# A two-layer encoder in one kernel: the PSUM banks of the first Strassen sums, two late steps, and the first loads

## The chip, the cores and the metric

The kernel runs as one program on one core of a Trainium2 chip. The metric is device time in microseconds (us) of one execution, taken as the median of the runs. The core's engines have their own instruction queues and run side by side: TensorE (PE, with PEld for its weight loads) multiplies, ScalarE (ACT) and VectorE (DVE) do the elementwise work, GpSimd (POOL) and SyncE (SP) mostly issue transfers (DMAs). PE writes its results into PSUM, which the kernel uses as eight banks of 128 x 512 floats; ACT and DVE read them there. Within an engine the instructions run in the order in which they stand; between engines they wait on semaphores.

## The reference

The input is `x` (256 tokens, 2048 features), with 256 memory tokens `mem`. Two layers follow each other. In each, one input projection feeds 12 mixer heads and 4 heads that attend to the memory; the outputs are concatenated, projected by `w_o` and added to `x`; then a squared-ReLU MLP of width 8192 is added.

```
m = rms_norm(mem, mem_norm); h = x
for i in range(2):
    n = rms_norm(h, attn_norm[i]);  z = n @ w_in[i]
    mix = neighbourhood_attention(q, k, v, rpb)      # layer 0
        | gqa_block_attention(rope(norm(q)), rope(norm(k)), v)   # layer 1
    km, vm = split(m @ w_mem_kv[i]);  cross = memory_attention(qm, km, vm)
    h = h + concat([mix, cross]) @ w_o[i]
    n = rms_norm(h, mlp_norm[i])
    h = h + square(relu(n @ w_up[i])) @ w_down[i]
return rms_norm(h, final_norm)
```

Everything is float32 in and out.

## The kernel before

**Arithmetic.** Every operand of a matmul is split into a rounded high part and the rest (`split`, L301 to L304: ACT copies into the high part, DVE subtracts for the low part), and a product is the sum of high x high, high x low and low x high. So each weight, once loaded, costs an ACT and a DVE instruction before PE can use it.

**Chunks and grains.** The weights come in chunks of 1 MB (128 x 2048 floats). The list `plan` holds the chunks in the order of use; `halves_of` turns each into two grains, `run_all` runs through the grains. A grain has up to three preparing stages (load, pre, prep) which are emitted some grains ahead of its products. `later(n, ...)` puts an emission off by n grains ("ticks"). Emission gives priority only: a scheduler then lays the instructions of each engine in the order in which, by its own timeline, their inputs are ready, so that a step emitted later need not end up later in its queue. `pin` and `past` (with `issue_after`) hold an order by hand.

**The head.** `begin` (L227) treats the first three chunks (columns of `w_km0`, the memory keys of layer 0) specially. The memory (`memT`, 2 MB) is loaded in eight slices into the room of `h`, and the three chunks in four quarters each into the three buffers `raw` of the ring pool, all issued on SP (L115 to L125). ACT and DVE make `memT` hi and lo (L329, L330) and the chunks' `hi` and `lo`; PE runs the three chunks a quarter at a time (L221, L224). The fourth chunk and those after it are loaded by `prep` in `halves_of` (L157) into the ring's three buffers, as these come free. `x_load` later uses the two buffers with the tag `l4` of the pool `work` for x transposed.

**Attention.** `attention` emits three steps for each head: `attend` (scores, exponentials), `attend2` (transposes of the probabilities and their split into `pT`), `attend3` (the value product `av`, L392 to L394, split into `cat`). In layer 1 this is called by `b_q_done` for three blocks of four heads, with `w_o` right behind.

**Residual and guard.** `o_done` adds the output projection to `h` (`add`, L650) and sums the squares of the new columns (`squares`, L592). For the last 512 columns these two and `inv` (L638 to L641) come off the path: the MLP starts from a scale taken from the first three quarters, and `later(4 | 6 | 8, past, ...)` emits them within the first grains of the MLP.

**The MLP.** `w_up` runs in eight parts of eight 128-column chunks (`u_products`, L702 to L704). Part 0 takes its PSUM tiles from the pool `ps_acc` (four banks in turn) beside `ps_att` (the other four). Each result is read by a Relu on ACT (L756), squared (L757), and turned into the left factors of a Strassen product. From the first grain of part 1 on, the two pools are closed and `ps_sums` is opened over the same eight banks: one tile `up` for `ps_u`, and seven sums `p1` to `p7`. `down_grains` runs `w_down` with seven products a step: `FIRST` (p3, p1, p2; L816 to L818 out of `bh`, `bl`), then `SECOND` (p5, p7, p6, p4 out of `th`, `tl`). A sum's tile is taken from the pool when its first product is run, so the banks are given in the order up, p3, p1, p2, p5, p7, p6, p4. A tile placed in a bank waits for the last reader of the tile that had the bank before; the last tile of part 0 (its eighth chunk) lies in the second bank, the one that p3 gets.

Of the kernel before, what the change touches and what calls it, by code (L numbers as in the profile page):

```python
# [17 lines left out]
P = 128  # L18
# [55 lines left out]
def encoder_kernel(ctx: ExitStack, tc: tile.TileContext, t: dict, out: bass.AP):  # L74
# [44 lines left out]
    for j in range(8):  # L119
        s = slice(j * 512, (j + 1) * 512)  # L120
        nc.sync.dma_start(mem0[:, s], t["memT"][:, s])
        if j % 2 == 0:
            s = slice(j * 256, (j + 2) * 256)
            for c in range(FIRST_CHUNKS):
                nc.sync.dma_start(raws[c][:, s], t["w_km0"][c][:, s])  # L125
    ident = const.tile([P, P], F32, name="ident")
    ones = const.tile([P, P], F32, name="ones")
    nc.gpsimd.memset(ones, 1.0)
# [15 lines left out]
    def halves_of(w):  # L144

        tiles = {}

        def load():
            tiles["raw"] = loaded(w.src, "U")

        def prep_early(hf):
            tiles[hf] = half_of_side(tiles["raw"], hf, MOVING_AT)

        def prep(hf):
            if hf == 0:
                tiles["raw"] = at.ring.tile([P, CH], F32, tag="raw", bufs=3, name="raw")
                nc.sync.dma_start(tiles["raw"], w.src)  # L157
            tiles[hf] = new_half()
            split(*tiles[hf], tiles["raw"][:, hf * HALF : (hf + 1) * HALF])

        def run(hf):
            if hf == 0:
                w.start(w)
            hi, lo = tiles.pop(hf)
            if w.kind == "S":
                s_products(w, hf * (KT // 2), KT // 2, hi, lo)
            else:
                for i in range(NT):
                    m_products(w, w.first + 2 * hf, 2, i, hi, lo, w.begins and hf == 0, w.last and hf == 1)

        def after():
            if w.last:
                w.done(w)
            if w.early == "last":
                to_work()

        if w.early:
            return [Grain(lambda: run(0), None, load, None, lambda: prep_early(0), SOON),
                    Grain(lambda: run(1), after, None, None, lambda: prep_early(1), SOON)]
        return [Grain(lambda: run(0), None, None, None, lambda: prep(0)),  # L180
                Grain(lambda: run(1), after, None, None, lambda: prep(1))]
# [212 lines left out]
            nc.tensor.matmul(av[:, :SEQ], v(1, k), pT[:, 0, k, :], start=False, stop=k == NT - 1)  # L394
        split(cat[:, head, :SEQ], cat[:, head, SEQ:], av[:, :SEQ])

    def attention(jobs, at, gap=1, lag=1):

        def step(n, job, prev):
            qT, kT, bias, v, head, cat = job  # L400
            if n == 0:
                res = attend(qT, kT, bias)
            elif n == 1:
                res = attend2(prev)
            else:
                return attend3(prev, v, head, cat)
            results[n, head] = res

        results = {}
        for t in range(len(jobs) + 2):  # L410
            for n in range(3):
                if 0 <= t - n < len(jobs):
                    j = t - n
                    later(at + gap * j + lag * n,
                          lambda n=n, job=jobs[j]: step(n, job, results.get((n - 1, job[4]))))


# [191 lines left out]
    def o_done(layer, nb):  # L609
        which = 2 * layer  # L610

        def guard():

            box["near"] = mean_square(which, GUARD, "near")
            box["scale"] = keep.tile([P, NT], F32, tag="scale", name="scale")
            nc.gpsimd.tensor_tensor(box["scale"], box["near"], mhalf[:, :NT], op=ALU.pow)
            box["hT"] = wide(f"hT{layer}")

        def begun():

            y = at.side.tile([P, NT, 512], F32, tag="T", bufs=2, name="h_s")
            for i in range(NT):
                nc.scalar.activation(y[:, i, :], h[:, i, D - 512 :], AF.Copy, scale=box["scale"][:, i : i + 1])
            box["begun"] = y

        def scaled(b):
            y = at.side.tile([P, NT, 512], F32, tag="T", bufs=2, name="h_s")
            for i in range(NT):
                nc.scalar.activation(y[:, i, :], h[:, i, b * 512 : (b + 1) * 512], AF.Copy,
                                     scale=box["scale"][:, i : i + 1])  # L630
            transposed(box["hT"], lambda i, k: y[:, i, k % 4 * P : (k % 4 + 1) * P],
                       list(range(b * 4, b * 4 + 4)), (G_M0, G_M1)[layer])

        def inv():

            v = mean_square(which, 4, "full")
            box["inv"] = keep.tile([P, NT], F32, tag="inv", name="inv")
            nc.vector.reciprocal(v, v)  # L638
            nc.vector.tensor_tensor(box["inv"], v, box["near"], op=ALU.mult)
            box["ninv"] = keep.tile([P, NT], F32, tag="ninv", name="ninv")  # L640
            nc.vector.tensor_scalar(box["ninv"], box["inv"], -1.0, None, op0=ALU.mult)  # L641

        def f(w):
            if nb == 0:
                closed("work")
                at.side = opened("side", side="right")
            def add():
                for i in range(NT):
                    hs = h[:, i, nb * 512 : (nb + 1) * 512]
                    nc.vector.tensor_tensor(hs, w.ps[i], hs, op=ALU.add)  # L650

            def squares():
                for i in range(NT):
                    sum_squares(which, i, nb)

            if nb < 3:
                add()
                squares()
            if nb == GUARD - 1:
                later(1, guard)  # L660
                for b in range(GUARD):
                    later(2 + 2 * b, scaled, b)
                later(7, begun)
            if nb == 3:
                y = box["begun"]
                for i in range(NT):
                    nc.vector.scalar_tensor_tensor(y[:, i, :], w.ps[i], box["scale"][:, i : i + 1], y[:, i, :],
                                                   op0=ALU.mult, op1=ALU.add)
                box["ready"] = transposed(box["hT"], lambda i, k: y[:, i, k % 4 * P : (k % 4 + 1) * P],
                                          list(range(12, KT)), (G_M0, G_M1)[layer])  # L670
                later(4, past, add)
                later(6, past, squares)
                later(8, past, inv)
        return f

    def add_o(layer):
# [40 lines left out]
    def up_grains(layer, part, m):  # L717
# [8 lines left out]
        def run(hf):  # L726
            if hf == 0:
                if part == 0:
                    own["ps"] = at.acc.tile([P, 512], F32, tag="acc", name="ps_u")[:, :SEQ]
                else:  # L730
                    if part == 1 and m == 0:
                        closed("ps_att", "ps_acc")
                        at.sums = opened("ps_sums", space=bass.MemoryType.PSUM)
                        box["ps"] = {}
                    own["ps"] = at.sums.tile([P, 512], F32, tag="up", name="ps_u")[:, :SEQ]
            u_products(own["ps"], hf * (KT // 2), KT // 2, *own.pop(hf))

# [35 lines left out]
    def down_grains(layer, part, n, begins, ends):  # L773
# [35 lines left out]
        def run(which, products):  # L809
            hi, lo = own.pop(which)  # L810
            a = box["a", part, j]
            for name, ai, bi in products:
                if begins:
                    box["ps"][name] = at.sums.tile([P, 512], F32, tag=name, name=name)
                ps, s = box["ps"][name], slice(bi * 512, (bi + 1) * 512)
                nc.tensor.matmul(ps, a[:, 0, ai, :], hi[:, s], start=begins, stop=False)  # L816
                nc.tensor.matmul(ps, a[:, 0, ai, :], lo[:, s], start=False, stop=False)  # L817
                nc.tensor.matmul(ps, a[:, 1, ai, :], hi[:, s], start=False, stop=ends)  # L818
# [6 lines left out]
        def after_second():  # L825
# [3 lines left out]
            if ends and (part, n) in FOLDS:  # L829
                folded(q)  # L830

        return [Grain(lambda: run("first", FIRST), lambda: after(FIRST), load, behind(pre), behind(prep_first), SOON),
                Grain(lambda: run("second", SECOND), after_second, None, None, behind(prep_second), SOON)]

    def columns_of(i, q, b):
        return h[:, i, q * 1024 + b * 512 : q * 1024 + (b + 1) * 512]
# [225 lines left out]
    def b_q_done(blk):  # L1062
        def f(w):
            outs = normed_heads(w)
            qT = at.work.tile([P, 4, 512], F32R, tag="l4", name="qT1")
            later(1, heads_T, outs, 4, qT)
            kvs = [(blk * 4 + j) // (NH // NKV) for j in range(4)]
            attention([(qT[:, j, :], box["kT"][:, kv, :], None, head_of(box["vb"], kv), blk * 4 + j, box["cat"])
                       for j, kv in enumerate(kvs)], 1, 2, 3)
        return f  # L1070

    def b_qm_done(w):
# [164 lines left out]
```

## Time and profile before

| What | us |
|---|---|
| median of 3 runs (2053.45 to 2055.89) | 2055.51 |
| the profiled execution, its own time | 2053.93 |
| its span, first to last instruction | 2052.1 |
| PE busy | 2029.9 (99%) |
| DVE busy | 1669.2 (81%) |
| ACT busy | 1252.7 (61%) |
| POOL busy | 119.3 (6%) |

The profiled execution lies 1.6 us under the median and within the runs; 1.8 us of its time lie outside the span. PE is busy nearly all the time, so what matters are the few places in which it stands still. A row of a timeline gives the start and the duration in us, the engine, the line, the operation, out<-in, the shape, how many, and in brackets how long the engine had been idle before and what ended that. A row of the chain gives start, length and what the chain went through. A row of the waits gives the engine and line that waited, whom for, and the total, the number of times and the longest wait. Matmuls overlap and their ends are modelled, so a loss on PE is best taken from start to start: in steady state a matmul with 512 columns starts 0.23 us after the one before, with 256 columns 0.11 to 0.12 us.

### The profile page before, as it was taken

To read this page: it belongs to the slowest core of one execution; us is meant where nothing else is said; L and a number is where in the kernel's file an instruction comes from. 1 tells how busy PE (TensorE), PEld (TensorE's weight loads), DVE (VectorE), ACT (ScalarE), POOL (GpSimd) and SP (SyncE) were. 2 spreads that over 40 slices of the span, in tenths; PEclk is the share of its full clock that TensorE was granted. 3 is DMA by queue.
4 is the path that set the end of the run, shared out by engine and by line. 5 is a ranking of instruction groups with operands and counts; after the bars stand their busy time and mean duration, and the time that the engine had idled before them with its cause. 6 is when DMAs were issued, how large, how long until landed. Compare 5 with 4: busy or idle time off the path is not lost.

```text
span 2052.1 us, 31583 instructions
## 1 busy us (share of the span) xinstructions
PE 2029.9 (99%) x12516; PEld 1812.2 (88%) x12516; DVE 1669.2 (81%) x2061; ACT 1252.7 (61%) x1652; POOL 119.3 (6%) x144
## 2 busy tenths in 40 slices
PE   8999999999999999999999999999999999999998
PEld 7888888889999999999988888889999999999996
DVE  6767666558998999989897667657988999999896
ACT  6755555556666666666656557556666666666664
POOL 0000000000000000000000001000000000000000
PEclk9999999999999999999999999999999999999999
DMA  7755555727777777787765554536877787887773
GB/s 280 283 190 179 188 176 171 276 88 223 231 231 231 221 237 230 220 243 224 225 218 205 176 180 144 194 116 221 242 226 231 217 238 221 237 229 224 235 219 135
DMA packets 93429, 433.79 MB, mean 211 GB/s; under 512 B 10464, under 2 KB 12128, under 8 KB 60128
## 3 DMA queue, kind: packets, MB, share of 16 engines
q1 hardware_dynamic: 75888, 399.25, 57.7%
q0 software_dynamic: 16816, 31.46, 8.7%
q8 instruction: 98, 1.61, 0.3%
q10 hardware_dynamic: 576, 1.05, 0.1%
q14 instruction: 51, 0.42, 0.1%
HBM read 398.17 MB, written 4.19 MB: 196 GB/s over the span
## 4 chain that ended last, share of the span: by engine, by line
PE 97%; ACT 1%; DVE 1%; issue 0%; DMA 0%; SPq 0%; POOLq 0%; POOL 0%; ACTq 0%
PE ps_u L704 11%; PE ps_u L702 11%; PE ps_u L703 11%; PE p L816 9%; PE p L817 9%; PE p L818 9%; PE ps_m L208 8%; PE ps_m L211 8%; PE ps_m L212 8%; PE ps_s L221 6%; PE ps_s L224 3%; PE pt_a L384 1%; PE pt_n L321 1%; DMA raw<-in_w_km 0%; PE av L392 0%
## 5 line engine op out<-in xcount | busy, mean ns | idle before, releaser
L704 PE MATMUL ps_u<-hT,ul 128*128 128x256 f32 x2048 | 568.4, 278 | 1.8 <-DVE ul L304 1.8
L702 PE MATMUL ps_u<-hT,uh 128*128 128x256 f32 x2048 | 568.6, 278 | 0.2
L703 PE MATMUL ps_u<-hT,uh 128*128 128x256 f32 x2048 | 567.9, 277 | 0.0
L303 ACT ACTIVATE uh<-raw_U 128x1024 fp32r<-128x1024 f32 x278 | 294.8, 1061 | 315.8 <-PE ps_u L703 294.8
L304 DVE TENSOR_TENSOR lo<-raw,hi 128x1024 fp32r<-128x1024 f32 (+1 forms) x224 | 266.4, 1195 | 161.7 <-ACT hi L303 158.4
L702 PEld LDWEIGHTS ps_u<-hT,uh 128*128 128x128 f32 x2048 | 384.9, 188 | 5.8 <-ACT uh L303 0.6
L704 PEld LDWEIGHTS ps_u<-hT,ul 128*128 128x128 f32 x2048 | 385.9, 189 | 3.7 <-DVE ul L304 2.6
L703 PEld LDWEIGHTS ps_u<-hT,uh 128*128 128x128 f32 x2048 | 384.4, 188 | 4.5
L304 DVE TENSOR_TENSOR ul<-raw_U,uh 128x1024 fp32r<-128x1024 f32 x278 | 337.6, 1219 | 40.5 <-ACT uh L303 40.4
L303 ACT ACTIVATE hi<-raw 128x1024 fp32r<-128x1024 f32 (+1 forms) x224 | 231.7, 1039 | 210.4 <-PE ps_m L212 117.8
L303 ACT ACTIVATE th<-t 128x2048 fp32r<-128x2048 f32 x112 | 215.1, 1920 | 123.5 <-PE p L818 117.1
L304 DVE TENSOR_TENSOR tl<-t,th 128x2048 fp32r<-128x2048 f32 x112 | 256.3, 2288 | 34.5 <-ACT th L303 34.1
L304 DVE TENSOR_TENSOR bl<-b,bh 128x1536 fp32r<-128x1536 f32 x112 | 196.1, 1751 | 0.3 <-ACT bh L303 0.2
L817 PE MATMUL p<-tl,a_s 128*128 128x512 f32 x448 | 177.2, 395 | 0.0
L818 PE MATMUL p<-th,a_s 128*128 128x512 f32 x448 | 174.4, 389 | 0.0
L303 ACT ACTIVATE bh<-b 128x1536 fp32r<-128x1536 f32 x112 | 166.2, 1484 | 10.2 <-PE p L818 4.0
L816 PE MATMUL p<-th,a_s 128*128 128x512 f32 x448 | 166.1, 395 | 0.0
L796 POOL DMA_DIRECT2D t<-b x112 | 97.1, 867 | 1164.5 <-DVE t L795 510.3
L221 PE MATMUL ps_s<-nT,hi 128*128 128x512 f32 x448 | 142.5, 397 | 0.0
L818 PE MATMUL p<-bh,a_s 128*128 128x512 f32 x336 | 131.1, 390 | 0.0
L817 PE MATMUL p<-bl,a_s 128*128 128x512 f32 x336 | 130.9, 390 | 0.0
L795 DVE TENSOR_TENSOR t<-t,b 128x512 f32<-128x512 f32 x112 | 77.2, 689 | 50.8 <-DMA t<-in_w_pair 43.7
(237 smaller groups left out, 3508.2 us busy)
## 6 DMA issues: line engine op xcount, KB each, us to landing
raw_U<-in_w_up SPq DMA_DIRECT2D x128, 1024.0 KB, 6.6
b<-in_w_pair SPq DMA_DIRECT2D x112, 768.0 KB, 4.5
raw<-in_w_o SPq DMA_DIRECT2D x32, 1024.0 KB, 5.0
t<-in_w_pair SPq DMA_DIRECT2D x112, 256.0 KB, 3.4
t<-b POOLq DMA_DIRECT2D x112, 256.0 KB, 6.7
raw<-in_w_b SPq DMA_DIRECT2D x21, 1024.0 KB, 4.9
raw<-in_w_av SPq DMA_DIRECT2D x12, 1024.0 KB, 4.9
raw<-in_w_aq SPq DMA_DIRECT2D x12, 1024.0 KB, 4.9
```

The costliest lines, as they stand in the source:

```text
L208: first = nc.tensor.matmul(w.ps[i], ah, hi[:, s], start=st, stop=False)
L211: nc.tensor.matmul(w.ps[i], ah, lo[:, s], start=False, stop=False)
L212: nc.tensor.matmul(w.ps[i], al, hi[:, s], start=False, stop=sp)
L221: nc.tensor.matmul(ps, hi[:, s], acts[:, k0 + j, :], start=k0 + j == 0, stop=False)
L303: first = nc.scalar.activation(dst_hi, src, AF.Copy)
L304: return first, nc.vector.tensor_tensor(dst_lo, src, dst_hi.bitcast(F32), op=ALU.subtract)
L702: nc.tensor.matmul(ps, hi[:, s], acts[:, k, :SEQ], start=k == 0, stop=False)
L703: nc.tensor.matmul(ps, hi[:, s], acts[:, k, SEQ:], start=False, stop=False)
L704: nc.tensor.matmul(ps, lo[:, s], acts[:, k, :SEQ], start=False, stop=k == KT - 1)
L816: nc.tensor.matmul(ps, a[:, 0, ai, :], hi[:, s], start=begins, stop=False)
L817: nc.tensor.matmul(ps, a[:, 0, ai, :], lo[:, s], start=False, stop=False)
L818: nc.tensor.matmul(ps, a[:, 1, ai, :], hi[:, s], start=False, stop=ends)
```

## The change

Four edits.

1. The first quarter of the three first chunks is issued on ACT's queue instead of SP's.
2. Two more chunks, the fourth of `w_km0` and the first of `w_vm0`, are loaded whole right behind the first loads, into the two `l4` buffers of the pool `work`; `prep` takes them from there.
3. The last residual columns, their squares and `inv` are emitted 4 ticks later in both layers, and in layer 1 the value product of the last head of the third block is emitted one tick later (`rest` is 0, 0 and 1 for the blocks 0, 1 and 2).
4. The banks of the seven sums are given at the first use of any: p4, p3, p1, p2, p5, p7, p6 behind `up`, so that p4 gets the second bank and each of the others the next one.

```diff
             for c in range(FIRST_CHUNKS):
-                nc.sync.dma_start(raws[c][:, s], t["w_km0"][c][:, s])
+                (nc.sync if j else nc.scalar).dma_start(raws[c][:, s], t["w_km0"][c][:, s])
+
+    soon = {}
+    for c, src in ((FIRST_CHUNKS, t["w_km0"][3]), (FIRST_CHUNKS + 1, t["w_vm0"][0])):
+        soon[c] = at.work.tile([P, CH], F32, tag="l4", name="raw_l4")
+        nc.sync.dma_start(soon[c], src)
...
             if hf == 0:
-                tiles["raw"] = at.ring.tile([P, CH], F32, tag="raw", bufs=3, name="raw")
-                nc.sync.dma_start(tiles["raw"], w.src)
+                n = plan.index(w)
+                if n in soon:
+                    tiles["raw"] = soon.pop(n)
+                else:
+                    tiles["raw"] = at.ring.tile([P, CH], F32, tag="raw", bufs=3, name="raw")
+                    nc.sync.dma_start(tiles["raw"], w.src)
...
-    def attention(jobs, at, gap=1, lag=1):
+    def attention(jobs, at, gap=1, lag=1, rest=0):
...
-                    later(at + gap * j + lag * n,
+                    more = rest if n == 2 and j == len(jobs) - 1 else 0
+                    later(at + gap * j + lag * n + more,
...
-                later(4, past, add)
-                later(6, past, squares)
-                later(8, past, inv)
+                later(8, past, add)
+                later(10, past, squares)
+                later(12, past, inv)
...
                 if begins:
-                    box["ps"][name] = at.sums.tile([P, 512], F32, tag=name, name=name)
+                    sum_of(name)
...
+    def sum_of(name):
+
+        if not box["ps"]:
+            for x in ("p4", "p3", "p1", "p2", "p5", "p7", "p6"):
+                box["ps"][x] = at.sums.tile([P, 512], F32, tag=x, name=x)
+                box["unused"].add(x)
+        if name in box["unused"]:
+            box["unused"].remove(name)
+        else:
+            box["ps"][name] = at.sums.tile([P, 512], F32, tag=name, name=name)
...
-                       for j, kv in enumerate(kvs)], 1, 2, 3)
+                       for j, kv in enumerate(kvs)], 1, 2, 3, blk // 2)
```

More of the change, by code (lines that the diff above doesn't have):

```diff
@@ L734, in run @@
                         box["ps"] = {}
+                        box["unused"] = set()
                     own["ps"] = at.sums.tile([P, 512], F32, tag="up", name="ps_u")[:, :SEQ]
```

## The prediction

> **What bounds the kernel now.** I read the page first, then the waits of PE, then PE's timeline around each wait, then ACT's beside it.
>
> The page's first and fourth parts:
>
> ```profile
> PE 2029.9 (99%) x12516; PEld 1812.2 (88%) x12516; DVE 1669.2 (81%) x2061; ACT 1252.7 (61%) x1652; POOL 119.3 (6%) x144
> PE 97%; ACT 1%; DVE 1%; issue 0%; DMA 0%; SPq 0%; POOLq 0%; POOL 0%; ACTq 0%
> ```
>
> PE is the chain. No edit here takes a matmul away, so the change can only win where PE stands still. PE's waits over the whole execution (columns: who waited for whom, total, times, longest):
>
> ```profile
> PE ps_s L221 <- ACT hi L303: 7.7, 2, 6.8
> PE p L816 <- ACT c L756: 2.1, 2, 1.1
> PE ps_u L704 <- DVE ul L304: 1.8, 3, 0.8
> PE av L392 <- ACT pT L303: 1.0, 1, 1.0
> ```
>
> Twice at the first sum p3 (L816), once at a value product, 6.8 us at the start and 0.9 us later in the head. PE's timeline at the first p3 wait and at the end of the head, and the same p3 row in layer 1:
>
> ```profile
> 488.97 0.28 PE L703 MATMUL ps_u<-hT,uh 128*128 128x256 f32 x1
> 490.31 0.50 PE L816 MATMUL p<-bh,a_s 128*128 128x512 f32 x1 [1.06 <-ACT c L756]
> 490.65 0.39 PE L817 MATMUL p<-bl,a_s 128*128 128x512 f32 x1
> ...
> 24.86 0.40 PE L224 MATMUL ps_s<-memT,lo 128*128 128x256 f32 x2
> 26.13 0.73 PE L221 MATMUL ps_s<-memT,hi 128*128 128x512 f32 x2 [0.87 <-ACT hi L303]
> 27.39 0.50 PE L224 MATMUL ps_s<-memT,lo 128*128 128x256 f32 x2 [0.52 <-DVE lo L304]
> ...
> 1421.79 0.50 PE L816 MATMUL p<-bh,a_s 128*128 128x512 f32 x1 [1.08 <-ACT c L756]
> ```
>
> And ACT's at the p3 wait, where the releaser stands:
>
> ```profile
> 483.80 0.36 ACT L756 ACTIVATE c<-ps_u 128x256 f32<-128x256 f32 x1
> ...
> 488.93 1.06 ACT L303 ACTIVATE uh<-raw_U 128x1024 fp32r<-128x1024 f32 x1 [0.23 <-PE ps_u L703]
> 489.90 0.37 ACT L756 ACTIVATE c<-ps_u 128x256 f32<-128x256 f32 x1
> ```
>
> The Relu of the last chunk of part 0 comes only at 489.90, because ACT's queue has a split before it (488.93) that itself waits for PE. p3 lies in the bank that this Relu reads. The Relu of the chunk before was over at 484.16.
>
> **The banks.** After the change p3 gets the third bank, whose last reader is that earlier Relu. So p3 starts when PE comes to it. From start to start 490.31 - 488.97 = 1.34 us, of which 0.11 is a normal step; the first matmul after the stall then takes 0.34 instead of 0.23 to the next. Gain 1.23 + 0.11 = 1.34 us. In layer 1 the last L703 starts at 1420.44, p3 at 1421.79, the next at 1422.13: 1.35 - 0.11 + 0.11 = 1.35. Sum 2.69.
>
> What is late next? p4 takes over the wait. It is the seventh product: after p3 at 489.08, six products of three matmuls at 0.23 us each put it at 493.2, and the Relu ends at 490.27: 2.9 us to spare. `bh` and `bl` were made at 478.36 and 479.86 and end by 481.62. `th` is over at 486.92, `tl` at 486.95 + 2.29 = 489.24, and is needed at 491.2. The next `ul` (489.16 + 1.22 = 490.38) is needed after the seven products, at 493.5; the one after it (491.90 + 1.22 = 493.12) 2.7 us later. All of these have more than 1.3 us, so nothing takes the stall back. Where ACT itself waits for PE (uh at 497.38), it moves with PE.
>
> **The two early chunks.** Before, the fourth chunk could be issued only when its ring buffer came free, at 19.88, and landed 5.05 us later at 24.93; PE ran out at 24.98. From start to start it loses 26.13 - 24.98 - 0.12 = 1.03 and, waiting for `lo`, 27.39 - 26.46 - 0.23 = 0.70; the two restarts cost 0.11 and 0.10 more. Together 1.94. Now it is issued behind the last slice of the memory (before at 13.73, landed 18.87), into a free buffer. The rate of such transfers is seen in the next two chunks, which land at 28.66 and 31.19, 2.5 us apart: so it lands near 18.9 + 2.5 = 21.4, its successor near 24. ACT was idle for 3.52 us up to 24.35 and splits it there; 1.06 and 1.22 us for a half give `hi` and `lo` by 23.7. It is wanted at about 24.7. I take the whole 1.94; the low end is 0, if it landed no earlier than before, and the point where it begins to cost is a landing at 22.4. The second early chunk is wanted 5.5 us later. The x transposed needs the same `l4` buffers, but is issued only at 60.22, long after both are split. The ring's three loads move up by two chunks; the bias rows now stand behind them on SP; they had been issued at 21.68 and are used behind the whole memory part.
>
> **The first quarter on ACT's queue.** Three issues leave SP (1.64, 2.11 and 2.58 us before) and come to ACT at 0.73 or so, at about 0.45 us each, ahead of its table load (1.28 us), which thus ends near 3.3 instead of 2.0; ACT then waits for data as it did till 4.50. SP's later slices of the memory move up by 1.4 us in issue. PE's start needs `hi` of the first chunk, then `memT` hi on ACT and lo on DVE. The scheduler now puts `hi` ahead of `memT` on ACT, and `lo` ahead of `memT` lo on DVE. From the rows: `hi` 0.66, then `memT` 0.46 on ACT; `lo` 0.68 and `memT` lo 0.44 on DVE, which make about 1.85 us from landing to PE when both have landed, against 0.70 before (6.08 to 6.78), when memory had landed at 4.41.
> - Early end: the chunk lands 2.9 us after issue, as the 256 KB stores on ACT's queue do at the end of the kernel (2041.32 to 2044.18): 3.6; the memory at 4.41 as before. `memT` hi is done at 4.9, lo at 5.4, PE starts at 5.5: a gain of 1.25.
> - Late end: the two share the engines and both land at 6.08, when the chunk landed before. PE starts at 7.95: a loss of 1.2.
> - Taken: by the packets of before, the 552 KB of the gains and both transfers had been moved by 5.0, though the last stragglers came later. With the chunk issued 0.9 us earlier I take 4.6 for both, a start at 6.5, a gain of 0.3, near the middle of the two ends.
>
> [...] After the start PE needs 18.2 us to the fourth chunk (6.78 to 24.98) whatever came before, as its quarters take 4.1 us and five slices of 0.65 us land in 3.3.
>
> **The late steps.** I cost the residual columns and the value product at nothing. The orders of instructions of both built programs agree on PE, ACT, DVE, POOL and SP, instruction for instruction, behind the first quarters of the head; only the waits of the seven sums differ. The adds were fillers and stay where they were (449.22 on DVE, L650). If they did move, the stalls to be won would be those of PE at 451.67 and 452.93 (0.26 and 0.92 us, about the same in layer 1) and at 1319.65 (1.14): at most 3.5 us. The loss is bounded by nothing, as no position changes.
>
> **Sum.** 1.34 + 1.35 + 1.94 + 0.3 + 0 = 4.9 us off the profiled execution's 2053.93: 2049.0. The median of the runs is 1.6 above that execution; against it I forecast 2055.5 - 4.9 = 2050.6, or 0.24% less. A measurement of this kernel can tell about 0.2%, 4.1 us, from no change.
>
> **Rivals.**
> - Shared start: the first transfers of both queues hold each other up, the chunk and the memory land between 5 and 6.1, PE starts at 7 to 7.95. For it: between 4.0 and 4.75 the engines moved only 20 to 44 KB in a quarter of a microsecond, so the start isn't at full rate even for one queue. Against it: at the end of the kernel two queues' stores land together in 2.7 to 2.9 us. Sum 3.4 to 4.4, time 2051.1 to 2052.1.
> - The stall is given back: DVE is busy for 13.23 of the 14 us from 482 to 496, so a PE that is 1.3 us ahead may meet a late `ul`. Against it the margins above, 2.5 us and more. Then the two bank gains go, and 2.2 us are left: 2053.3.
> - The late steps act after all: 4.9 + 3.5 = 8.4, 2047.1. Only the scheduler's order speaks, and against it.
> - Slower: the six first transfers (three of each queue) finish together, not in turn. Before, 1.5 MB had landed at 9.79. Then `hi` and the rest give a PE start of 9.79 + 1.85 = 11.65, 4.9 later than before; against 4.6 won elsewhere, 0.3 slower, 2055.8. It decides from a landing at 9.5 on. Against it: on one queue the transfers landed in their order, 0.65 us apart.
>
> **How the numbers follow.** Forecast (start between 5.5 and 7.0): 0.65. Shared start 0.20, of which a part still reaches 4.1. Given back 0.06, late steps 0.05, slower 0.04. Faster by over 0.2%: nearly all of the forecast, the late steps and a quarter of the shared start, less some for the scatter of the runs: 0.67. Slower by over 0.2% needs the last rival and more: 0.02. Within: 0.31. Range: the early end (4.9 - 0.3 + 1.25 = 5.9) taken off the profiled execution's 2053.9 gives 2048.0. The late end (4.9 - 0.3 - 1.2 = 3.4) off the slowest run, 2055.9, gives 2052.5, and a fourth chunk that lands 0.7 us too late, or half of the bank gains given back, 2053.2.
>
> **What would show it.** L816 gone from PE's waits for L756; p4 without a wait; no wait of L221 or L224 near 25; the fourth chunk landed before 22.4; PE's first matmul before 6.8; the waits at 451 and 1319 still there, 5 us earlier. I am wrong if PE's first matmul comes after 7.3, or if a `ul` or `tl` wait appears behind p3.

## The result, and the profile after

The changed kernel took 2050.91 us (median of 18 runs, 2048.8 to 2053.46) against 2054.53 for the kernel before (18 runs): a ratio of 0.9983, with a 95% interval of 0.9976 to 0.9989, or 3.6 us less. Run again (e9 below), it gave 2050.18 against 2054.94: 0.9979 (0.9971 to 0.9988), 4.8 us less. The forecast was 2050.6, 4.9 us less than before.

The profiled execution took 2051.05 us with a span of 2049.3 (before: 2053.93 and 2052.1). The first and fourth parts of its page, busy time by engine and the chain:

```profile
PE 2029.9 (99%) x12516; PEld 1813.1 (88%) x12516; DVE 1669.0 (81%) x2061; ACT 1252.6 (61%) x1652; POOL 119.3 (6%) x144
PE 98%; DVE 0%; ACT 0%; issue 0%; DMA 0%; POOLq 0%; POOL 0%; SPq 0%; ACTq 0%
```

PE's busy time is the same to a tenth. What changed is its waits (who waited for whom, total, times, longest); lines of the code lie 9 to 12 further down, so L816 is now L828, L221 is L230, L704 is L715:

```profile
PE ps_s L230 <- DVE memT L339: 7.6, 1, 7.6
PE ps_u L715 <- DVE ul L313: 1.8, 3, 0.8
PE av L401 <- ACT pT L312: 1.0, 1, 1.0
```

The wait of the first sum for the Relu (2.1 us) is gone, and so are the two waits near 25. The wait of the value product stands as it was. But the wait at the start has grown from 6.8 to 7.6 us, and it is now for `memT`, not for `hi`. PE's timeline at the start, at 25 and at the first sum:

```profile
7.55 1.65 PE L230 MATMUL ps_s<-memT,hi 128*128 128x512 f32 x3 [7.55 <-DVE memT L339]
10.28 2.33 PE L230 MATMUL ps_s<-memT,hi 128*128 128x512 f32 x5
...
24.77 0.85 PE L230 MATMUL ps_s<-memT,hi 128*128 128x512 f32 x3
25.46 0.40 PE L233 MATMUL ps_s<-memT,lo 128*128 128x256 f32 x2
...
489.73 0.28 PE L714 MATMUL ps_u<-hT,uh 128*128 128x256 f32 x1
489.85 0.39 PE L828 MATMUL p<-bh,a_s 128*128 128x512 f32 x1
```

At 489.85 p3 follows the `ps_u` product before it by a normal 0.12 us. ACT runs the Relu that p3 used to wait for only at 490.66, 0.8 us after p3 has begun:

```profile
490.66 0.37 ACT L768 ACTIVATE c<-ps_u 128x256 f32<-128x256 f32 x1
```

And ACT's timeline of the start:

```profile
4.67 0.63 ACT L312 ACTIVATE hi<-raw 128x512 fp32r<-128x512 f32 x1 [1.03 <-DMA raw<-in_w_km]
6.47 0.91 ACT L338 ACTIVATE memT<-h,gains 128x256 fp32r<-128x256 f32 x2 [1.18 <-DMA h<-in_memT]
```

The chunk's first quarter is there at 4.64, early as meant, but the memory's first slice lands only at 6.38; before it had landed at 4.41, and `memT` hi had begun at 4.50. The rows of before, ACT's and PE's:

```profile
4.50 0.91 ACT L329 ACTIVATE memT<-h,gains 128x256 fp32r<-128x256 f32 x2 [2.28 <-DMA h<-in_memT]
6.78 2.08 PE L221 MATMUL ps_s<-memT,hi 128*128 128x512 f32 x4 [6.78 <-ACT hi L303]
```

Laid matmul for matmul beside the profile of before, the 2.85 us of the span come together so:

| Where | us, after less before |
|---|---|
| first matmul, 6.78 to 7.55 | +0.77 |
| longer stretch at half speed behind it (0.43 us for 512 columns, as at 10.28, in place of 0.23) | +1.00 |
| the two stalls near 25 | -1.93 |
| part 0 of `w_up`, layer 0: steps of 118 instead of 113 ns, and its `ul` waits | +0.92 |
| p3's wait, layer 0 | -1.36 |
| part 0 of `w_up`, layer 1: steps of 113 instead of 118 ns, and its `ul` waits | -0.93 |
| p3's wait, layer 1 | -1.33 |
| rest | +0.01 |

The three gains are as forecast. The start isn't, and the second, fourth and sixth rows belong to no step of the prediction.

### The profile page after: what moved, and what is told of

Same layout as the page of the kernel before. It is cut to its first block, busy times and chain, and to the rows that moved or that the text cites. A ratio compares the mean times of both kernels' runs of the same rounds, so it can differ in the third digit from the quotient of the medians.

```text
span 2049.3 us, 31582 instructions
## 1 busy us (share of the span) xinstructions
PE 2029.9 (99%) x12516; PEld 1813.1 (88%) x12516; DVE 1669.0 (81%) x2061; ACT 1252.6 (61%) x1652; POOL 119.3 (6%) x144
## 4 chain that ended last, share of the span: by engine, by line
PE 98%; DVE 0%; ACT 0%; issue 0%; DMA 0%; POOLq 0%; POOL 0%; SPq 0%; ACTq 0%
PE ps_u L715 11%; PE ps_u L713 11%; PE ps_u L714 11%; PE p L828 9%; PE p L829 9%; PE p L830 9%; PE ps_m L217 8%; PE ps_m L220 8%; PE ps_m L221 8%; PE ps_s L230 7%; PE ps_s L233 3%; PE pt_a L393 1%; PE pt_n L330 1%; PE av L401 0%; PE sc_ps L367 0%
## 5 line engine op out<-in xcount | busy, mean ns | idle before, releaser
L715 PE MATMUL ps_u<-hT,ul 128*128 128x256 f32 x2048 | 568.4, 278 | 1.8 <-DVE ul L313 1.8
L313 DVE TENSOR_TENSOR lo<-raw,hi 128x1024 fp32r<-128x1024 f32 (+1 forms) x220 | 261.4, 1194 | 164.6 <-ACT hi L312 162.1
L715 PEld LDWEIGHTS ps_u<-hT,ul 128*128 128x128 f32 x2048 | 386.0, 189 | 3.6 <-DVE ul L313 2.6
L312 ACT ACTIVATE hi<-raw 128x1024 fp32r<-128x1024 f32 (+1 forms) x220 | 227.5, 1039 | 210.2 <-PE ps_m L221 119.0
L828 PE MATMUL p<-th,a_s 128*128 128x512 f32 x448 | 166.1, 395 | 0.0
L230 PE MATMUL ps_s<-nT,hi 128*128 128x512 f32 x448 | 142.5, 397 | 0.0
```

The source lines that it names most:

```text
L230: nc.tensor.matmul(ps, hi[:, s], acts[:, k0 + j, :], start=k0 + j == 0, stop=False)
L312: first = nc.scalar.activation(dst_hi, src, AF.Copy)
L313: return first, nc.vector.tensor_tensor(dst_lo, src, dst_hi.bitcast(F32), op=ALU.subtract)
L715: nc.tensor.matmul(ps, lo[:, s], acts[:, k, :SEQ], start=False, stop=k == KT - 1)
```

## The experiments

The first theory from this comparison: the three gains stand, each in its own place; the first quarters on ACT's queue delay the memory's slice and with it PE's start; the later steps do nothing. Rivals: the early chunks delay the start, or the start is hidden by the stall at 25 in any case. "SP-only" below means that no load is issued on ACT's queue.

| Run | median us | ratio to before (95%) | first matmul |
|---|---|---|---|
| e1 banks alone | 2051.85 | 0.9987 (0.9978 to 0.9995) | 6.51 |
| e2 early chunks alone | 2051.92 | 0.9988 (0.9979 to 0.9997) | 6.49 |
| e3 ACT's queue alone | 2053.23 | 0.9995 (0.9986 to 1.0004) | 7.60 |
| e4 changed kernel, SP-only | 2050.06 | 0.9975 (0.9964 to 0.9985) | 6.55 |
| e5 late steps alone | 2054.53 | 0.9998 (0.9989 to 1.0007) | 6.57 |
| e6 SP-only, dummy matmuls | 2049.14 | 0.9971 (0.9960 to 0.9982) | 6.66 |
| e7 changed kernel, dummy matmuls | 2050.56 | 0.9980 (0.9971 to 0.9990) | 7.79 |
| e8 one quarter on ACT's queue | 2050.11 | 0.9978 (0.9968 to 0.9988) | 6.53 |
| e9 changed kernel again | 2050.18 | 0.9979 (0.9971 to 0.9988) | 7.61 |
| e10 second bank to p1 | 2055.62 | 1.0002 (0.9994 to 1.0011) | 7.63 |
| e11 halves first, dummies | 2050.99 | 0.9980 (0.9971 to 0.9989) | 5.27 |
| e12 slice first, dummies | 2048.62 | 0.9964 (0.9950 to 0.9978) | 6.21 |

### e1, the banks alone

```diff
-                    box["ps"][name] = at.sums.tile([P, 512], F32, tag=name, name=name)
+                    sum_of(name)
```

> Only the banks of the seven sums are reordered. Theory (each part of the change is worth what stands in its own place): both waits of L816 for the Relu go, 1.34 and 1.35 us from start to start, so 2.7 us less than before, with PE's first matmul at 6.78 and the stalls near 25 as they were. Rival (the two bank gains are given back by later ul or tl): under 1 us less, with new waits of the ul products in layer 0 after 486.

Matmul for matmul, p3's stalls gave 1.32 us in layer 0 and 1.33 in layer 1. PE's waits of this run:

```profile
PE ps_s L221 <- ACT hi L303: 7.4, 2, 6.5
PE ps_u L704 <- DVE ul L304: 1.8, 3, 0.8
```

The `ul` waits are the 1.8 us of before: nothing is given back. The theory holds. PE began at 6.51, not 6.78, though nothing was changed there; such starts without an edit varied by some 0.3 us (6.49 in e2 to 6.78 before).

### e2, the early chunks alone

```diff
+        soon[c] = at.work.tile([P, CH], F32, tag="l4", name="raw_l4")
+        nc.sync.dma_start(soon[c], src)
```

> Only the two early chunks, with all first loads on SP's queue. Theory: the two waits at 24.98 and 26.46 go, the fourth chunk lands near 21.4, 1.9 us less than before, start of PE at 6.78 as before. Rival (the two early chunks are what delays the start, as they are in flight with the first loads): the first matmul comes at about 7.5, and only 0.2 to 1.2 us are won.

The fourth chunk landed at 21.23, and 1.91 us went between the last matmul before the stalls and the end of them. PE began at 6.49, so the early chunks do not delay the start. But from the start to 25 this execution lost 0.74 us to a longer stretch at half speed, so that its span fell by 1.45 only.

### e3, ACT's queue alone

```diff
-                nc.sync.dma_start(raws[c][:, s], t["w_km0"][c][:, s])
+                (nc.sync if j else nc.scalar).dma_start(raws[c][:, s], t["w_km0"][c][:, s])
```

> Only the first quarters of the three chunks on ACT's queue. Theory (the two queues share the engines, and the memory's first slice loses by it): first matmul near 7.5, memory's first slice landed near 6.4, 0.8 us slower than before, and 1.8 us slower if the longer stretch of half-speed matmuls at the start belongs to it. Rival (the prediction's step): start at 6.5, 0.3 us faster. Second rival (the fourth chunk's landing at 24.93 sets the end of the head, so that the start is hidden): no change.

The start came as the theory has it: first matmul at 7.60, memory's slice at 6.43, and 1.81 us late just before 25. Yet behind the head the kernel stood 0.12 us ahead of before. ACT's timeline:

```profile
23.80 1.06 ACT L303 ACTIVATE hi<-raw 128x1024 fp32r<-128x1024 f32 x1 [3.44 <-DMA raw<-in_w_km]
```

The fourth chunk was issued at 18.83 and landed at 23.70 (before 19.88 and 24.93), and PE wanted it only at 26.91. So the stall of 1.93 us near 25 vanished by itself and took the whole loss. Alone the edit costs nothing, by the second rival: the stall hides the start. Once the early chunks have removed that stall, there is no cover.

### e4, the changed kernel without the ACT queue

```diff
-                (nc.sync if j else nc.scalar).dma_start(raws[c][:, s], t["w_km0"][c][:, s])
+                nc.sync.dma_start(raws[c][:, s], t["w_km0"][c][:, s])
```

> The changed kernel with the first quarters of the three chunks back on SP's queue; the other three edits stay. Theory: first matmul back at 6.78, 4.6 us less than before (1.34 + 1.35 + 1.94), which is 0.8 to 1.8 us less than the changed kernel. Rival (the late start came from the two early chunks or from the order on the engines): no better than the changed kernel, 2.9 to 3.6 us less than before, with the first matmul at about 7.5 still.

The first matmul is back at 6.55 and the memory's slice at 4.40; 1.0 to 1.1 us earlier than in the changed kernel. The span is 3.93 us under that of before. In time the two could not be told apart: 0.9975 against 0.9983 and 0.9979, with intervals that overlap. The place of the loss is shown; its size in the whole is only bounded, and e7 narrows it.

### e5, the late steps alone

```diff
-                later(4, past, add)
-                later(6, past, squares)
-                later(8, past, inv)
+                later(8, past, add)
+                later(10, past, squares)
+                later(12, past, inv)
```

> Only the later emission of the last residual columns, their squares, inv and the one value product. Theory (the order of instructions on every engine stays the same): no change, with PE's waits at 451, 453 and 1319.65 as before. Rival (they act after all): up to 3.5 us less than before, and the waits at those places gone or shorter.

No change, and the waits stand: those of `ul` 1.8 us, that of the value product 1.0. In part 0 this execution ran at 118 ns a step in layer 0 and at 113 in layer 1, the execution of before the other way round, though the order of instructions is the same.

### e6 and e7, PE kept busy before the data comes

```diff
     nc.gpsimd.memset(ones, 1.0)
+    idle = at.att.tile([P, 512], F32, tag="att", name="idle")
+    for _ in range(12):
+        nc.tensor.matmul(idle[:, :P], ones, ones, start=True, stop=True)
```

> All first loads on SP's queue as in the run without the first edit, and 12 matmuls of ones with ones into a tile that nobody reads are put ahead of everything on PE, from about 1.0 us on. Theory (PE runs at half speed until it has been busy for some microseconds, whatever it computes): the half-speed stretch after the first loads, which lost about 0.1 us for every 256 columns, 1.5 us in the profile of before and 2.4 in that of the run without the first edit, is gone or nearly so; 1.5 to 2.4 us less than without the dummies, some 6 less than before. Rival (the slow start belongs to the first matmuls on real data or to the loads in flight): the first matmuls still step at 427 ns for 512 columns, no gain. Second rival (the dummies run into the first real matmul): start later than 6.6.

PE's timeline in e6 (the dummies are 24 passes):

```profile
0.98 4.36 PE L136 MATMUL idle<-ones 128*128 128x128 f32 x24 [0.98 <-POOL mhalf L138]
6.66 1.46 PE L233 MATMUL ps_s<-memT,hi 128*128 128x512 f32 x4 [1.32 <-ACT hi L315]
...
9.46 1.20 PE L233 MATMUL ps_s<-memT,hi 128*128 128x512 f32 x4 [0.16 <-DVE memT L342]
```

Four matmuls from 6.66 take 1.46 us; in e4 the same four take 2.07:

```profile
6.55 2.07 PE L230 MATMUL ps_s<-memT,hi 128*128 128x512 f32 x4 [6.55 <-ACT hi L312]
```

The dummies themselves stepped at 213 ns until 3.9 and at 112 from then on. What the steps up to 24 us have over 117 ns for every 256 columns fell from 2.4 us in e4 to 0.7. None of these 0.7 is half speed: 0.33 is a new wait at 9.46 for the memory's second slice, landed at 8.35, and the rest are restarts and short waits. With a start 0.1 us later the head gained 1.54. Theory held, its size less a new wait.

> The changed kernel with the same 12 dummy matmuls. Theory: with the half-speed stretch out of the way, what the first quarters on ACT's queue cost is the later start alone: first matmul near 7.55 against 6.55, so 1.0 us more than the run with dummies and all loads on SP's queue. Rival (the length of the half-speed stretch is a matter of the queue used): no difference between the two but the start's own, and the stretch stays here.

Here the first matmul came at 7.79, at full speed as well (the first three took 1.13 us, against 1.65 in the changed kernel; 0.2 us over the normal steps, all told). Behind the head this run stands 0.62 us behind e6, which started 1.13 us earlier but waited at 9.46. So what ACT's queue costs is 0.6 us in these two executions, where the loads bind the first quarter, and up to the 1.1 of the later start where PE does. The medians, 2050.56 and 2049.14, do not tell the two kernels apart: their intervals overlap. The half-speed stretch is no part of it.

### e8, one quarter on ACT's queue

```diff
-                (nc.sync if j else nc.scalar).dma_start(raws[c][:, s], t["w_km0"][c][:, s])
+                (nc.scalar if j + c == 0 else nc.sync).dma_start(raws[c][:, s], t["w_km0"][c][:, s])
```

> The changed kernel with only the first chunk's first quarter on ACT's queue; those of the second and third chunk go back to SP's. Theory (what held the memory's first slice up to 6.38 were the 512 KB of the second and third quarter beside it): only gains, one slice and one quarter, 552 KB, are ahead, both land near 5.0 to 5.3, memT hi and lo follow in 0.5 and 0.5, and PE starts at 6.2 to 6.5, no later than with all on SP's queue. Rival (a second queue at the start delays SP's slice whatever it carries): the memory lands at 6 or later and PE starts at 7.2 or later.

ACT's timeline:

```profile
4.62 0.63 ACT L312 ACTIVATE hi<-raw 128x512 fp32r<-128x512 f32 x1 [1.95 <-DMA raw<-in_w_km]
5.45 0.91 ACT L338 ACTIVATE memT<-h,gains 128x256 fp32r<-128x256 f32 x2 [0.20 <-DMA h<-in_memT]
```

The slice landed at 5.36 and PE began at 6.53. With none, one and three quarters on ACT's queue the memory's slice lands at 4.40, 5.36 and 6.38 to 6.62. An estimate: at the 0.65 us that a 256 KB transfer takes later in the same load, three quarters are 1.95 us, and 4.40 + 1.95 = 6.35, near the measured landings; one quarter would give 5.05, but 5.36 was measured. So the slice pays roughly for what is in flight beside it on ACT's queue, in the single quarter's case for more, and it is the 2nd and 3rd quarter that make ACT's queue a loss. With one it is neither loss nor gain: what the chunk wins (4.59 for 5.85) the slice loses.

### e9, the changed kernel again

> The changed kernel itself, beside the next two on the same chip. Theory: first matmul at 7.5 to 7.8, memory's first slice landed at 6.4 to 6.7, as in its first profile and in the other two runs with three quarters on ACT's queue; 3.6 us less than before. In layer 0's part 0 and layer 1's the 256-column steps of w_up take 113 or 118 ns whichever the execution falls into (if it is the program's: 118 in layer 0, 113 in layer 1 again).

First matmul at 7.61, slice at 6.43. PE's timeline, to be held against the row at 10.28 above:

```profile
10.33 1.55 PE L230 MATMUL ps_s<-memT,hi 128*128 128x512 f32 x5
```

The same five matmuls of the same program: 1.55 us here, 2.33 there. Half speed lasted 3.2 us in this execution and 5.3 in the first; the losses were 1.5 and 2.5. So the +1.00 in the table above is not the edit's. Nor are the rows of part 0: here layer 0 ran at 113 ns and layer 1 at 118, in the first profile it was the other way.

### e10, the second bank to the second sum

```diff
-            for x in ("p4", "p3", "p1", "p2", "p5", "p7", "p6"):
+            for x in ("p1", "p3", "p4", "p2", "p5", "p7", "p6"):
```

> The changed kernel, but the second bank, in which part 0's last tile lies, goes to p1, the second product, in place of p4. Theory (the wait is that for the last Relu on this one bank, and it ends at a fixed time): p1 comes three matmuls, 0.69 us, behind p3, so of the 1.34 us of each layer 0.65 come back, 1.3 us more than the changed kernel, with a wait of about 0.4 us at L829 or L828 for the Relu in both layers. Rival (what helped was taking the seven banks at once, not which sum has the second): no wait, no difference.

PE's timeline in layer 0, at the first sums and, 579 us later, behind `w_down`:

```profile
487.79 0.40 PE L828 MATMUL p<-bh,a_s 128*128 128x512 f32 x1
489.03 0.50 PE L828 MATMUL p<-bh,a_s 128*128 128x512 f32 x1 [0.37 <-ACT c L768]
...
1067.32 0.39 PE L221 MATMUL ps_m<-uh,a_p 128*128 128x512 f32 x1
1068.96 0.50 PE L217 MATMUL ps_m<-uh,a_p 128*128 128x512 f32 x1 [1.25 <-DVE h L862]
```

The bank wait came back as worked out: 0.62 us in layer 0 and 0.65 in layer 1 for 0.65 each. But the kernel lost 5.4 us against e9, not 1.3. The other end of the pool paid: behind `w_down` a tile `ps_m` takes over a bank of the sums and waits for the add into `h` that reads it last, 1.57 us more in layer 0 and 1.55 in layer 1. A further 1.6 us of the profiled execution lie in `tl` waits between 1862 and 1889, which e3's profile has too (2.4 us) and the changed kernel's have not; their cause stays open. Which sum has which bank thus has a price where the pool opens and one where it closes. The change's own order pays at neither.

### e11 and e12, an earlier start

For e11 the first slice and quarter are loaded and split in halves (ten dummies), and the second slice comes next; e12 keeps them whole, with that same order and the 12 dummies:

```diff
+    for s in (slice(0, 256), slice(256, 512)):
+        nc.sync.dma_start(mem0[:, s], t["memT"][:, s])
+        nc.sync.dma_start(raws[0][:, s], t["w_km0"][0][:, s])
+    nc.sync.dma_start(mem0[:, 512:1024], t["memT"][:, 512:1024])
```

> No load on ACT's queue; ten dummy matmuls; the first slice of the memory and the first quarter of the first chunk are loaded and split in two halves each, in turn, and the second slice of the memory comes ahead of the second and third chunk. Theory (PE's start is set by the bytes ahead of its first operands, 40 + 128 + 128 KB in place of 552): first matmul near 5.3, and no wait at 9.46 for the second slice, which lands near 6.7 in place of 8.35; 0.7 us less than with the dummies alone, in all some 5.5 to 7 us less than before. Rival (the first loads have a fixed latency, or the loads' rate binds the whole head): start 6 or later, or waits inside the first quarter that give it back; no better than with the dummies alone.

PE's timeline of e11:

```profile
5.27 1.20 PE L238 MATMUL ps_s<-memT,hi 128*128 128x512 f32 x2
7.71 0.51 PE L238 MATMUL ps_s<-memT,hi 128*128 128x512 f32 x1 [0.88 <-DVE memT L349]
9.29 1.05 PE L238 MATMUL ps_s<-memT,hi 128*128 128x512 f32 x3 [1.08 <-ACT hi L322]
```

The start is at 5.27, as the bytes had it, and worth nothing. PE was at half speed till about 6.6, then waited twice for the next loads. Its steps from 9.29 on were at full speed, but at 10.0 it fell back to half speed, till 13.4 (two matmuls of 512 columns took 0.86 us from 10.56 to 11.42, and 0.47 from 13.50 on): the granted clock is 1.00 from 6.7 to 9.9, 0.50 from 10.1 to 13.3 and 1.00 again from 13.5. Of the 4.7 us that the steps have over 117 ns for every 256 columns, the two waits are 2.5 and half speed most of the rest. So the clock was won and lost again behind a stretch of 3.2 us in which PE was busy for 1.25. Behind the head this run stood 2.5 us behind e6.

> No load on ACT's queue, 12 dummy matmuls, and the memory's second slice comes right behind the first chunk's first quarter, ahead of the second and third chunk. Theory (with the clock at full speed, the first quarter waits for the second slice, which landed at 8.35): the slice lands near 6.7, the wait before the third chunk's matmuls at 9.46 goes, the first matmul stays near 6.6 and the first quarter ends 0.4 to 0.7 us earlier than with the dummies alone: some 6.5 us less than before. Rival (the wait only moves to the second chunk, which now lands later): no gain, and if the gaps are long, half-speed matmuls again.

The second slice landed at 6.74, but the third chunk's quarter at 9.32, and the wait moved to it:

```profile
10.02 0.73 PE L237 MATMUL ps_s<-memT,hi 128*128 128x512 f32 x2 [0.58 <-ACT hi L319]
```

The head ended 0.8 us later than in e6, so the theory fell and the rival held. The medians of e6 (7 runs) and e12 (5 runs), from different chips, are nevertheless the lowest of all. Both are under before beyond their intervals. Against the changed kernel the ratios, 0.9971 and 0.9964 for 0.9983 and 0.9979, speak for 1.6 to 3.9 us, with intervals that overlap; the profiles put the gain in the head, at 1.7 to 2.6 us for e6 and 0.9 to 1.8 for e12.

## Why the prediction was right, and where not

- **Banks, 1.34 + 1.35.** Right: 1.36 and 1.33, and 1.32 and 1.33 alone (e1). A slip without effect: as part 0 takes four banks in turn and its eighth chunk lies in the second, the third bank, which p3 got, held the fifth chunk, not the seventh; its Relu was over earlier still. p4 took over the bank without a wait, as the margin of 2.9 us had it; e10 shows that a sum 0.69 us behind p3 would have met the Relu. One question was never asked: what the new order does where the pool closes. There it happened to cost nothing, but e10's order costs 1.6 us a layer.
- **Early chunks, 1.94.** Right: 1.93, and 1.91 alone. The landing was forecast at 21.4 and came at 21.34.
- **First quarter on ACT's queue, +0.3.** Wrong, and the sign with it: the start came 0.8 us later than in the profile of before, 1.0 to 1.1 later than in the other SP-only profiles. The step that failed is the 552 KB taken to be ahead of the start, and from it the landing of both at 4.6. It counted one quarter beside the gains and the slice, but all three quarters were in flight with the slice, and SP's next loads too. The packets begun by 5.0 us held 664 KB, 406 of them on ACT's queue, and the slice was still short. It landed at 6.38, the chunk at 4.64. e8, with one quarter on ACT's queue, did start at 6.53, the forecast's 6.5, but by another way: its slice landed at 5.36, not 4.6, and from there to PE it took 1.17 us, not 1.85, because `hi` was done by then. That agreement is luck. So the shared-start rival came true, and the mark set for being wrong (first matmul after 7.3) was passed. The early edge of that rival, landings at 5 and a start at 7, is shown by no run: with three quarters on ACT's queue the slice landed at 6.38 to 6.62 and PE began at 7.55 to 7.79. What the two queues did to each other at the start is seen on the slice: issued at 1.17 both times, it landed at 4.41 with all loads on SP's queue and at 6.38 with three quarters on ACT's.
- **Late steps, 0.** Right (e5).
- **Given back, and slower.** Neither came: the `ul` waits stayed at 1.8 us and no `tl` waits appeared behind p3; the slice landed far from 9.5.
- **The sum.** With the start at its measured cost the terms give 1.34 + 1.35 + 1.94 - 0.8 = 3.8, against 3.6 and 4.8 measured. The forecast of 4.9 was 1.1 too high by its own terms. That its time, 2050.6, lies within 0.5 us of both medians is luck: it was counted off a median of 3 runs, 2055.51, and the kernel before came out at 2054.53 and 2054.94 over more runs, which takes back 0.6 to 1.0 of the 1.1. What it held likeliest, faster by over 0.2%, came out at 0.17% and then 0.21%. The working also left out a scatter: half speed at the start costs 1.3 to 2.5 us by the execution, and part 0's two step lengths about 1.25 us a layer, of which some 0.3 came back at the next `ul` wait.

## What to carry to other kernels

Three transfers put on a second queue at the start were paid for here by what the first matmul still waited for (the memory's slice landed at 6.38 in place of 4.41, and the start came 0.8 us later): count all bytes in flight on all queues, not those of the operand that moved. An edit that costs nothing while a later stall covers it gets its price when another edit removes the stall (here 0.6 us between the profiles of e6 and e7), so price the parts in each other's company. And a new order of banks has to be followed to both ends of its pool.

## What the runs showed that was not expected

- **Half speed at the start.** PE's first matmuls on data took 427 ns for 512 columns in place of about 233, for 2.7 to 5.3 us, in all runs without dummies; two executions of the changed kernel had 5.3 and 3.2. The dummies were slow for 2.9 us in e6 and for all of their 5.5 in e7. So the length varied with the execution; what ends such a stretch was not shown.
- **Full speed was lost again.** In e11 PE fell back to half speed for 3.4 us; none of its pauses before that was longer than 1.1 us.
- **It need not be paid on data.** Matmuls of ones did as well. In e7 all 24 passes were slow, and the first matmuls on data, 1.3 us after the last of them, were fast (three in 1.13 us, against 1.65 in the changed kernel). What the dummies gain is shown in the head of the profiles; between the medians of e6 and e4 the intervals overlap.
- **Two step lengths.** With 256 columns in part 0 of `w_up`, PE steps at 113 or at 118 ns, keeps to one for up to 32 us, and was seen to change only around a stall. Both occur in the same program, in either layer. What chooses is open.
